# A mixture of experts whose scattered rows are gated first and added to one row of each token

## The chip, the cores and the metric

The kernel runs on one core of a Trainium2 chip. The metric is the device time of one execution, in microseconds (us). The core has TensorE (PE in the rows; PEld is its weight load), VectorE (DVE), ScalarE (ACT) and GpSimd (POOL), and SyncE (SP), which here only issues transfers. All transfers run on the core's 16 DMA engines.

## The reference, cut to what matters

One decoder layer: 512 tokens of 1024 numbers, two attention branches, and then 32 experts, of which each token takes 4. All the change lies in the experts' part:

```python
logits = xf @ w_router + b_router            # 512 x 32
vals, idx = lax.top_k(logits, 4)
gate = softmax(vals)                         # 512 x 4
# for every token and each of its 4 experts e:
up = x @ w_up[e] + b_up[e]                   # 2048 numbers: glu, lin
act = min(glu, 7) * sigmoid(1.702 * min(glu, 7)) * (clip(lin, -7, 7) + 1)
y = act @ w_down[e] + b_down[e]              # 1024 numbers
moe[token] += gate * y
out = x_mid + rmsnorm(moe) * g * (gate of the modulation)   # float32
```

## The kernel before, in words

**Stages.** Up to about 430 us attention, the router and the tables of places. Then a pipeline over 32 experts: at step i the up product of expert i (8 tiles of w_up, 1 MB each) and the down product of expert i-1 (4 tiles of w_down, 1 MB each). At the end the rows of each token are put together, normed, added to `xm` and stored.

**Kinds of experts.** The experts but the first are ranked by their number of rows. `KINDS` gives each step a number of slots: S has 128, N has 64, X has both. S is multiplied in three passes: `wsplit` splits a weight tile into `whi` (ACT) and `wlo` (DVE, both line 110), and `mm_w` (lines 1133 to 1141) multiplies. N is multiplied in plain float32 straight from `raw` (lines 1204 and 1258). A step over a pair N, S is the common case.

**Weights.** `parts` (line 1438) keeps `raw` tiles coming on SP's queue, through 9 buffers of 1 MB (`rawtile`): a load waits until its buffer has been consumed.

**Places.** `indices` (line 1057) turns the tables into three columns for each slot of an expert: the token `ti`, the row `di = 4 ti + j` of the token's j-th choice, and for N the half row `dh`. `gather` (line 1098) fetches the tokens' rows from DRAM, `scatter` (line 1228) writes an expert's result to rows of `y4`, a DRAM tensor of 2048 rows x 1024 (8 MB), that `zero_y4` cleared earlier. Both are issued by POOL. All experts' scatters write rows of their own, and the program declares that none waits for another.

**The end.** The last expert's result isn't scattered first: its rows are put in place on TensorE with a one-hot matrix `oht` (line 1604). For each of four blocks of 128 tokens (`q`), `partial` (line 1538) reads 2 MB of `y4`, and adds the four rows of a token, each multiplied by its gate `g4` (ACT line 1552, DVE line 1554). `finish` (line 1564) squares and sums (ACT), multiplies with `gp2` (POOL line 1569), works out the reciprocal root with small DVE operations (`rstd_of`, lines 218 to 231), scales and adds `xm` (DVE line 1571) and stores. A loop behind it, for experts with more rows than slots, closes the program.

**Order.** From step 2 on, `tc.manual_schedule` makes PE, ACT, DVE and POOL follow the order in which the code is written; before step 2 and after the last up step a scheduler sets it. SP's queue always follows the order of the code.

Of the kernel before, what the change touches and what calls it, by code (L numbers as in the profile page):

```python
# [20 lines left out]
S = 512  # L21
# [96 lines left out]
def emit(tc, A, dbg=None, stop_at=99):  # L118
# [194 lines left out]
    y4 = dram.tile([S * 4, D], F32, name="y4")  # L313

    def zero_y4(z, part):
        for i in part:
            k.load(y4[512 * i:512 * i + 512, :].rearrange("(p a) (b n) -> p (a b) n", p=128, n=256),
                   z[:, None, :].to_broadcast([128, 16, 256]))
# [524 lines left out]
    with tc.issue_after(k.last.ins):  # L843
        zero_y4(zero, range(4))
# [113 lines left out]
    g4 = rt.tile([128, NQ, 4], F32, name="g4")  # L958
# [6 lines left out]
    tab = rt.tile([128, NQ, 3, 32], BF16, name="tab")  # L965
# [6 lines left out]
    def route(qs):  # L972
        n, sl = len(qs), slice(qs[0], qs[-1] + 1)
        for q in qs:
            nc.vector.scalar_tensor_tensor(lg[:, q, :], pls[q], rn[1, q], br_, op0=OP.mult, op1=OP.add)
        for q in qs:
            nc.vector.max(v8[:, q], lg[:, q])
        for q in qs:
            nc.vector.max_index(i8[:, q], v8[:, q], lg[:, q])
        nc.vector.tensor_copy(i4[:, sl], i8[:, sl, 0:4])  # L980

        eoh = k.sp.tile([128, 2, n, 32, 4], F32, name=f"eoh{qs[0]}", tag="eoh", bufs=1)
        for i, q in enumerate(qs):
            nc.vector.tensor_tensor(eoh[:, 0, i], cst[:, C_E:C_E + 32][:, :, None].to_broadcast([128, 32, 4]),
                                    i4[:, q, None, :].to_broadcast([128, 32, 4]), op=OP.is_equal)
# [4 lines left out]
        return last  # L990
# [52 lines left out]
    scat = []  # L1043
# [13 lines left out]
    def indices(sets, tag, late=False):  # L1057
# [11 lines left out]
        di = rt.tile([128, n], I32, name="di" + tag, tag="di", bufs=3)  # L1069

        dh = rt.tile([128, n], I32, name="dh" + tag, tag="dh", bufs=3)

        def rest():
            pz = pq.tile([128, n, 4], F32, name=f"slot{tag}", tag="t")
            for i, parts in enumerate(sets):
                for pos_, vals, a, b in parts:
                    for q in range(NQ):
                        nc.tensor.matmul(pz[a:b, i, 0:3], lhsT=ohs[i][:, q, a:b], rhs=vals[:, q], start=(q == 0),  # L1078
                                         stop=(q == 3))
            sv = rt.tile([128, n, 3], F32, name="sv" + tag, tag="sv", bufs=2)  # L1080
            nc.vector.tensor_copy(sv, pz[:, :, 0:3])  # L1081
            nc.vector.scalar_tensor_tensor(ti, sv[:, :, 0], float(OOB), sv[:, :, 1], op0=OP.add, op1=OP.add)
            nc.vector.scalar_tensor_tensor(di, ti, 4.0, sv[:, :, 2], op0=OP.mult, op1=OP.add)
            return nc.vector.tensor_scalar(dh, di, 2.0, half, op0=OP.mult, op1=OP.add)
        return ti, di, dh, rest if late else rest()
# [142 lines left out]
    def scatter(ys, di):  # L1228
        h = D // ys.shape[1]
        st = nc.gpsimd.indirect_dma_start(out=y4.rearrange("r (h n) -> (r h) n", h=h) if h > 1 else y4,  # L1230
                                          out_offset=bass.IndirectOffsetOnAxis(ap=di, axis=0), in_=ys,
                                          in_offset=None, bounds_check=S * 4 * h - 1, oob_is_err=False)
        for s_ in scat:
            tc.declare_no_dep(st.ins, s_.ins, reason="every expert writes rows of its own")
        scat.append(st)

    class Down:
# [5 lines left out]
        def tile(self, c, raw, w):  # L1243
# [19 lines left out]
            if an is not None:  # L1263
                yn = etile("yn", 512)
                nc.scalar.activation(yn, self.pn, AF.Copy)
                after_tiles(2, lambda: scatter(yn, self.dis[1]))
            if a:
# [6 lines left out]
                nc.scalar.activation(ys, flat(self.p), AF.Copy)  # L1274
                after_tiles(2, lambda: scatter(ys, self.dis[0]))
# [7 lines left out]
    def tables():  # L1283
# [5 lines left out]
        nc.gpsimd.tensor_copy(byx[:, :, 1], tab[:, :, 2])  # L1289
# [116 lines left out]
    def prep(some, late=False):  # L1406
# [11 lines left out]
        ti, di, dh, last = indices(sets, f"s{some[0]}", late)  # L1418
        for n, (i, b) in enumerate(own):
            idx.setdefault(i, [None, None])[b] = (ti[0:64, n:n + 1], dh[:, n:n + 1]) if b else (ti[:, n:n + 1], di[:, n:n + 1])  # L1420
# [17 lines left out]
    def parts():  # L1438
# [9 lines left out]
        return ready.pop(0)  # L1448

# [17 lines left out]
    for i, kd in enumerate(KINDS):  # L1467
# [29 lines left out]
        for n, (c, x) in enumerate(tiles(i)):  # L1497
# [24 lines left out]
        if i + 1 < E:  # L1522
            down = Down(up, [x and x[1] for x in idx[i]], tags[1])
    by_hand.close()
    tick(True)


    def gp2_rows():
        g = xg0
        for j in range(2):  # L1530
            pz = ptile("gp2", "t")
            for b in range(4):
                nc.tensor.transpose(pz[:, 0, b * 128:(b + 1) * 128],
                                    colp[:, 2, 4 * j + b:4 * j + b + 1].to_broadcast([128, 128]), ident)
            nc.scalar.activation(g[:, j * 512:(j + 1) * 512], pz[:, 0], AF.Copy)
        return g

    def partial(q, y, more=False):

        yv = y4[q * 512:(q + 1) * 512, :].rearrange("(p j) d -> p j d", j=4)  # L1540
        yl = []
        for i in range(2):
            t = rawtile([128, 2, D])
            if q == NQ - 1 and i == 1:
                k.load(t[:, 0], yv[:, 2])
                k.load(t[:, 1], yv[:, 3])
            else:
                k.load(t, yv[:, 2 * i:2 * i + 2])
            yl.append(t)
        for j in range(4):  # L1550
            if j == 0 and not more:
                nc.scalar.activation(y, yl[0][:, 0], AF.Copy, scale=g4[:, q, 0:1])
            else:
                nc.vector.scalar_tensor_tensor(y, yl[j // 2][:, j % 2], g4[:, q, j:j + 1], y, op0=OP.mult, op1=OP.add)

    yqs = []

    def ytile(i):
        if i % 2 == 0:
            nb[0] += 1  # L1560
            yqs[:] = [ep.tile([128, 2, D], F32, name=f"yq{nb[0]}", tag=f"t{ysl[i // 2]}")]
        return yqs[0][:, i % 2]

    def finish(q, y, nm):

# [117 lines left out]
```

## Time and profile before

| | us |
|---|---|
| runs shown: lowest, median, highest | 1554.36, 1557.8, 1560.94 |
| the profiled execution | 1553.92 |
| its span | 1552.1 |
| last down matmul to the span's end | 1504.7 to 1552.1 |
| first scatter, last scatter that the reads wait for | 505.3, 1491.7 |

The span runs from the first to the last instruction of the profiled execution; 1.8 us of its time lie around it. TensorE is busy for 91% of it, DVE for 57%, and the DMA queue of SP for 76.6% of 16 engines. No single share tells what ends a stage: the experts' part has both TensorE and the DMA engines near full, and the chain of waits says which of them ended last.

### The profile page before, as it was taken

To read this page: it belongs to the slowest core of one execution; us is meant where nothing else is said; L and a number is where in the kernel's file an instruction comes from. 1 tells how busy PE (TensorE), PEld (TensorE's weight loads), DVE (VectorE), ACT (ScalarE), POOL (GpSimd) and SP (SyncE) were. 2 spreads that over 40 slices of the span, in tenths; PEclk is the share of its full clock that TensorE was granted. 3 is DMA by queue.
4 is the path that set the end of the run, shared out by engine and by line. 5 is a ranking of instruction groups with operands and counts; after the bars stand their busy time and mean duration, and the time that the engine had idled before them with its cause. 6 is when DMAs were issued, how large, how long until landed. Compare 5 with 4: busy or idle time off the path is not lost.

```text
span 1552.1 us, 19027 instructions
## 1 busy us (share of the span) xinstructions
PE 1417.7 (91%) x6949; PEld 906.5 (58%) x6949; DVE 879.4 (57%) x1290; ACT 671.4 (43%) x826; POOL 158.9 (10%) x190
## 2 busy tenths in 40 slices
PE   7999999998868999999979999999999999899980
PEld 2788785576745656657435445756647556474550
DVE  2786747766877454736333343754736547463566
ACT  3545435465544443635232242543625526252441
POOL 0200020100342000000010110000000000000002
PEclk9999999999869999999999999999999999999995
DMA  8522137308676999999996999999999999999972
GB/s 299 169 82 82 56 129 274 139 28 271 244 248 263 376 404 420 411 412 411 420 404 240 385 376 419 416 416 419 416 414 415 415 406 417 405 391 415 420 303 104
DMA packets 101798, 494.17 MB, mean 318 GB/s; under 512 B 14353, under 2 KB 39418, under 8 KB 48579
## 3 DMA queue, kind: packets, MB, share of 16 engines
q1 hardware_dynamic: 93139, 472.12, 76.6%
q0 software_dynamic: 8560, 20.78, 3.8%
q8 instruction: 56, 0.92, 0.2%
q14 instruction: 43, 0.35, 0.1%
HBM read 474.50 MB, written 26.74 MB: 323 GB/s over the span
## 4 chain that ended last, share of the span: by engine, by line
PE 71%; DVE 12%; DMA 10%; ACT 5%; issue 2%; SPq 0%; ACTq 0%; DVEq 0%; POOLq 0%
PE un L1204 9%; PE dnn L1258 7%; DMA raw<-in_w_down_dram 6%; PE ug L1137 4%; PE ug L1139 4%; PE ul L1137 4%; PE ul L1139 4%; PE ug L1141 3%; PE ul L1141 3%; DVE wlo L110 3%; PE dn L1141 3%; PE dn L1137 3%; DMA raw<-in_w_up_dram 2%; PE dn L1139 2%; ACT whi L110 2%
## 5 line engine op out<-in xcount | busy, mean ns | idle before, releaser
L110 DVE TENSOR_TENSOR wlo<-raw,whi 128x2048 fp32r<-128x2048 f32 x180 | 408.2, 2291 | 130.9 <-ACT whi L110 130.4
L110 ACT ACTIVATE whi<-raw 128x2048 fp32r<-128x2048 f32 x180 | 342.5, 1914 | 125.6 <-PE ul L1139 41.9
L1204 PE MATMUL un<-raw,xn 128*64 128x512 f32 x1152 | 259.7, 599 | 0.0
L1204 PEld LDWEIGHTS un<-raw,xn 128*64 128x64 f32 x1152 | 79.2, 137 | 152.3 <-issue 151.3
L1258 PE MATMUL dnn<-raw,an 128*64 128x512 f32 x576 | 132.6, 599 | 2.2 <-DMA raw<-in_w_down_dram 2.2
L1141 PE MATMUL dn<-wlo,at 128*128 128x512 f32 x240 | 78.1, 407 | 10.3 <-DVE wlo L110 9.6
L110 ACT ACTIVATE xt<-xT 128x1024 fp32r<-128x1024 f32 x15 | 15.3, 1023 | 164.6 <-PE xT L1113 164.6
L1137 PE MATMUL ug<-whi,xt 128*128 128x512 f32 x240 | 79.4, 412 | 3.7 <-ACT whi L110 2.5
L1137 PE MATMUL dn<-whi,at 128*128 128x512 f32 x240 | 78.4, 408 | 3.2 <-ACT whi L110 2.7
L1258 PEld LDWEIGHTS dnn<-raw,an 128*64 128x64 f32 x576 | 37.7, 136 | 72.0 <-issue 64.6
L1081 DVE COPY svs<-slots 128x6 f32<-128x6 f32 (+2 forms) x17 | 2.8, 164 | 134.6 <-PE slots L1078 134.6
L1137 PE MATMUL ul<-whi,xt 128*128 128x512 f32 x240 | 77.2, 402 | 1.6 <-DVE ln L1175 1.6
L1141 PE MATMUL ug<-wlo,xt 128*128 128x512 f32 x240 | 76.0, 398 | 1.9 <-DVE wlo L110 1.9
L1139 PE MATMUL ug<-whi,xt 128*128 128x512 f32 x240 | 77.5, 404 | 0.0
L1139 PE MATMUL ul<-whi,xt 128*128 128x512 f32 x240 | 77.0, 402 | 0.0
L1139 PE MATMUL dn<-whi,at 128*128 128x512 f32 x240 | 75.6, 396 | 0.0
L1141 PE MATMUL ul<-wlo,xt 128*128 128x512 f32 x240 | 75.5, 396 | 0.0
L1099 POOL DMA_INDIRECT xg<-h2d,tis x33 | 37.0, 1121 | 364.6 <-PE xN L1124 219.2
L1174 DVE TENSOR_SCALAR l<-ul 128x1024 f32<-128x1024 f32 x15 | 18.3, 1223 | 86.2 <-PE ul L1146 86.2
L1141 PEld LDWEIGHTS dn<-wlo,at 128*128 128x128 f32 x240 | 43.2, 188 | 28.9 <-DVE wlo L110 20.2
L112 DVE SCALAR_TENSOR_TENSOR at<-aT,at 128x1024 fp32r<-128x1024 f32 x15 | 18.4, 1225 | 72.7 <-ACT at L111 72.7
L1137 PEld LDWEIGHTS dn<-whi,at 128*128 128x128 f32 x240 | 42.9, 189 | 24.0 <-ACT whi L110 11.2
(521 smaller groups left out, 2483.9 us busy)
## 6 DMA issues: line engine op xcount, KB each, us to landing
raw<-in_w_up_dram SPq DMA_DIRECT2D x256, 1024.0 KB, 17.4
raw<-in_w_down_dram SPq DMA_DIRECT2D x127, 1024.0 KB, 16.2
wada<-in_w_ada_dram SPq DMA_DIRECT2D x24, 1024.0 KB, 7.3
y<-zero SPq DMA_DIRECT2D x4, 2048.0 KB, 16.6
raw<-y SPq DMA_DIRECT2D x7, 1024.0 KB, 11.9
wor<-in_w_out_dram SPq DMA_DIRECT2D x4, 1024.0 KB, 6.0
x<-in_x_dram SPq DMA_DIRECT2D x8, 256.0 KB, 5.2
xm<-in_x_dram SPq DMA_DIRECT2D x4, 512.0 KB, 5.7
```

Source lines behind the costliest of these rows:

```text
L110: return (nc.scalar.activation(hi, src, AF.Copy), nc.vector.tensor_sub(lo, src, hi.bitcast(F32)))
L112: nc.vector.scalar_tensor_tensor(lo, src, scale, hi.bitcast(F32), op0=OP.mult, op1=OP.subtract))
L1081: nc.vector.tensor_copy(sv, pz[:, :, 0:3])
L1099: k.last = nc.gpsimd.indirect_dma_start(out=xg0[0:n], out_offset=None, in_=h2d, in_offset=bass.IndirectOffsetOnAxis(ap=ti[0:n], axis=0), b ...
L1137: nc.tensor.matmul(o, lhsT=xh, rhs=wh, start=first, stop=False)
L1139: nc.tensor.matmul(o, lhsT=xl, rhs=wh, start=False, stop=False)
L1141: nc.tensor.matmul(o, lhsT=xh, rhs=wl, start=False, stop=False)
L1174: nc.vector.tensor_scalar(l, pl_, 8.0, -6.0, op0=OP.min, op1=OP.max)
L1204: nc.tensor.matmul(self.pn[64 * c:64 * c + 64, a], lhsT=xn[:, kk, :], rhs=raw[:, o:o + 512], start=False, stop=kk == KT - 1, skip_group_ch ...
L1258: nc.tensor.matmul(self.pn[64 * n:64 * n + 64], lhsT=an[:, c % 2 * 2 + b, 64 * (c // 2):64 * (c // 2) + 64], rhs=raw[:, b, 512 * n:512 * n ...
```

## The change

Each token has one row in DRAM, `ytot` (512 x 1024, 2 MB), where it had four. ACT multiplies an expert's rows with their gates as it moves them out of PSUM, and the scattering transfer adds them to the row in DRAM (`compute_op=OP.add`). For that the gate travels through the tables: `tab` has five columns in place of three (the token's two parts, and the gate in three bf16 parts, `in_three`), and `indices` gives a column of gates `gs_`. The declaration that scatters don't wait for each other is gone: each waits for the one before. The end reads the 2 MB of `ytot` in four loads of 512 KB, and TensorE adds them, through the identity in float32, to the one-hot product of the last expert. ACT squares from PSUM, DVE multiplies from PSUM with the root and `gp2`, and adds `xm` in a second operation; POOL does nothing there. The one-hot matrix and `gp2` are made at the last up step's sixth tile. The hand-written order now covers the end, too.

```diff
-    y4 = dram.tile([S * 4, D], F32, name="y4")
+    ytot = dram.tile([S, D], F32, name="ytot")
+    def zero_y(z):
+        k.load(ytot.rearrange("(p a) (b n) -> p (a b) n", p=128, n=256), z[:, None, :].to_broadcast([128, 16, 256]))
...
-        zero_y4(zero, range(4))
+        zero_y(zero)
...
-        last = nc.vector.tensor_reduce(mb[:, sl], eoh[:, 0], op=OP.max, axis=AX.X)
-        nc.vector.tensor_tensor(eoh[:, 1].rearrange("p n e j -> p (n e) j"), eoh[:, 0].rearrange("p n e j -> p (n e) j"),
-                                cst[:, C_J:C_J + 4][:, None, :].to_broadcast([128, n * 32, 4]), op=OP.mult)
-        nc.vector.tensor_reduce(tab[:, sl, 2], eoh[:, 1], op=OP.max, axis=AX.X)
+        return nc.vector.tensor_reduce(mb[:, sl], eoh, op=OP.max, axis=AX.X)
...
+    nc.vector.tensor_tensor(gw, lg, v8[:, :, 0:1].to_broadcast([128, NQ, 32]), op=OP.subtract)
+    nc.scalar.activation(gw, gw, AF.Exp)
+    nc.vector.tensor_tensor(gw, gw, mb, op=OP.mult)
+    nc.vector.tensor_reduce(gs4, gw, op=OP.add, axis=AX.X)
     nc.vector.reciprocal(gs4, gs4)
+    nc.vector.tensor_tensor(gw, gw, gs4[:, :, None].to_broadcast([128, NQ, 32]), op=OP.mult)
+    def in_three(dst, src, r):
+        nc.vector.tensor_copy(dst[:, :, 0], src)
+        nc.vector.tensor_tensor(r, src, dst[:, :, 0], op=OP.subtract)
+        nc.vector.tensor_copy(dst[:, :, 1], r)
+        nc.vector.tensor_tensor(r, r, dst[:, :, 1], op=OP.subtract)
+        nc.vector.tensor_copy(dst[:, :, 2], r)
+    in_three(tab[:, :, 2:5], gw, gr)
...
-            nc.vector.scalar_tensor_tensor(di, ti, 4.0, sv[:, :, 2], op0=OP.mult, op1=OP.add)
-            return nc.vector.tensor_scalar(dh, di, 2.0, half, op0=OP.mult, op1=OP.add)
+            nc.vector.tensor_reduce(gs_, sv[:, :, 2:5], op=OP.add, axis=AX.X)
+            return nc.vector.tensor_scalar(dh, ti, 2.0, half, op0=OP.mult, op1=OP.add)
...
     def scatter(ys, di):
         h = D // ys.shape[1]
-        st = nc.gpsimd.indirect_dma_start(out=y4...,
-                                          bounds_check=S * 4 * h - 1, oob_is_err=False)
-        for s_ in scat:
-            tc.declare_no_dep(st.ins, s_.ins, reason="every expert writes rows of its own")
+        nc.gpsimd.indirect_dma_start(out=ytot...,
+                                     bounds_check=S * h - 1, oob_is_err=False, compute_op=OP.add)
...
-                nc.scalar.activation(ys, flat(self.p), AF.Copy)
-                after_tiles(2, lambda: scatter(ys, self.dis[0]))
+                nc.scalar.activation(ys, flat(self.p), AF.Copy, scale=self.dis[0][1])
+                after_tiles(2, lambda: scatter(ys, self.dis[0][0]))
...
+    def y_rows():
+        for q in range(NQ):
+            if q % 2 == 0:
+                t = rawtile([128, 2, D])
+            k.load(t[:, q % 2], ytot[q * 128:(q + 1) * 128, :])
+    def finish(q, y, nm, z, gp2):
+        nc.scalar.activation(z, y, AF.Square, accum_out=ssf)
+        r = rstd_of(ssf, D, f"rf{nm}{q}")
+        nc.vector.scalar_tensor_tensor(z, y, r, gp2, op0=OP.mult, op1=OP.mult)
+        nc.vector.tensor_tensor(z, z, xm[q], op=OP.add)
+        k.load(A["out"][0, q * 128:(q + 1) * 128, :], z)
...
+            if i == E - 1 and n == 5:
+                oht, gp2 = one_hots(), gp2_rows()
...
+    def first(q):
+        for n in range(2):
+            nc.tensor.matmul(pcs[q][:, n], lhsT=ident, rhs=ys[q][:, n * 512:(n + 1) * 512], start=True, stop=False)
+    for q in range(NQ - 1):
+        first(q)
+    for q in range(NQ):
+        if q == NQ - 1:
+            first(q)
+        for n in range(2):
+            for i in range(2):
+                nc.tensor.matmul(pcs[q][:, n], lhsT=oht[:, q], rhs=yr[:, i, n * 512:(n + 1) * 512], start=False, stop=(i == 1))
+    for q in range(NQ):
+        finish(q, flat(pcs[q]), "", ys[q], gp2)
+    by_hand.close()
+    scatter(yl, ti)
```

POOL's queue around the step of kind X, before. `xg` is a gather's tile, `y` and `yn` are what is scattered, and the brackets name what an instruction waits for (DMASW are semaphores of transfers that POOL issued).

```order
L1230 DMA y_380<-yn_6794,dhs_5820 4096x512 [waits Activation_49]
L1474 COPY cm_6984<-sel 128x128 [waits PE_49,Pool_49]
L1099 DMA xg_3889<-h2d,tis_6607 128x1024 [waits DMASW5_49,DMASW3_49]
L1230 DMA y_380<-yn_6978,dhs_6229 4096x512 [waits Activation_49]
L1230 DMA y_380<-y_6982,dis_6228 2048x1024 [waits DMASW7_49,Activation_49]
L1099 DMA xg_3889<-h2d,tis_7021 64x1024 [waits DMASW5_49,DVE_49,PE_49]
```

The same place in the changed kernel:

```order
L1235 DMA ytot<-yn_6804,dhs_5829 1024x512 [waits DMASW2_49,Activation_49]
L1515 COPY cm_6994<-sel 128x128 [waits PE_49,Pool_49]
L1104 DMA xg_3886<-h2d,tis_6617 128x1024 [waits DMASW3_49]
L1235 DMA ytot<-yn_6988,dhs_6238 1024x512 [waits DMASW4_49,Activation_49]
L1235 DMA ytot<-y_6992,tis_6237 512x1024 [waits DMASW6_49,Activation_49]
L1104 DMA xg_3886<-h2d,tis_7031 64x1024 [waits DMASW5_49,DVE_49,PE_49]
```

The instructions stand in the same order; what moved is the wait: every scatter now waits for a transfer of POOL's queue, too, the scatter before it.

DVE's queue during the first up step, before: `wlo` is the split of a weight tile, `svs` and `tis` lead to the second expert's gather.

```order
L110 TENSOR_TENSOR wlo_4452<-raw_3881,whi_4451 128x2048
L1330 TENSOR_SCALAR pos_4403<-pos_4403 128x4
L1065 TENSOR_TENSOR ohs_4425<-cst,pos_4403 128x4x64 x2
L1065 TENSOR_TENSOR ohs_4428<-cst,pos_4403 128x512
L110 TENSOR_TENSOR wlo_4468<-raw_3883,whi_4467 128x2048
L1081 COPY svs_4446<-slots_4433 128x6
L1065 TENSOR_TENSOR ohs_4642<-cst,pos_4403 128x4x64
L1082 SCALAR_TENSOR_TENSOR tis_4430<-svs_4446 128x2
```

The same stretch in the changed kernel:

```order
L1069 TENSOR_TENSOR ohs_4438<-cst,pos_4408 128x512
L1028 TENSOR_TENSOR gr<-gr,tab_4409 128x128
L110 TENSOR_TENSOR wlo_4478<-raw_3880,whi_4477 128x2048
L1029 CAST tab_4409<-gr 128x4x32
L110 TENSOR_TENSOR wlo_4494<-raw_3882,whi_4493 128x2048
L1085 COPY svs_4444<-slots_4443 128x10
L110 TENSOR_TENSOR wlo_4510<-raw_3884,whi_4509 128x2048
L1087 SCALAR_TENSOR_TENSOR tis_4440<-svs_4444 128x2
```

Two more splits of a weight tile stand ahead of `tis`, and the five operations of `in_three` are threaded between.

PE's queue after the last down matmul, in the changed kernel (`sum` are the PSUM tiles of the four blocks, `raw` the loaded rows of `ytot`, `cst` the identity):

```order
L1151 MATMUL dn_10750<-bt,sel 128x512 x2
L1586 MATMUL sum_10818<-raw_10781,cst 128x512 [waits DMAHW2_49]
L1586 MATMUL sum_10818<-raw_10781,cst 128x512
L1586 MATMUL sum_10819<-raw_10781,cst 128x512 [waits DMAHW3_49]
L1586 MATMUL sum_10819<-raw_10781,cst 128x512
L1586 MATMUL sum_10820<-raw_10784,cst 128x512 [waits DMAHW4_49]
L1586 MATMUL sum_10820<-raw_10784,cst 128x512
L1594 MATMUL sum_10818<-yr,oht 128x512 [waits Activation_49]
```

Six float32 matmuls now stand between the last down matmul and the first one-hot matmul, which came right behind it before.


## Rows read from the trace of the kernel before

**Rows 1.** Page, 40 slices of 38.8 us: DMA engines' busy tenths.

```profile
DMA  8522137308676999999996999999999999999972
```

**Rows 2.** Windows: start, end, length, each engine's busy us, granted clock, DMA share, GB/s.

```profile
505.00:780.00 275.00, 267.78 (x1268) 160.54 (x1266) 138.79 (x104) 113.32 (x82) 19.98 (x23) 1.00 1.01 409
780.00:900.00 120.00, 108.37 (x485) 52.55 (x483) 39.45 (x32) 33.49 (x28) 13.45 (x11) 0.97 0.86 334
900.00:1436.00 536.00, 521.21 (x2451) 316.46 (x2449) 289.15 (x248) 233.83 (x164) 40.21 (x43) 1.00 1.01 412
```

**Rows 3.** Chain that ended last, experts' part: start, us, engine, work, records.

```profile
551.04 10.45 PE un L1204 x48
...
613.45 10.45 PE un L1204 x48
...
740.09 15.88 DMA raw<-in_w_down_dram
...
1081.42 14.78 DMA raw<-in_w_down_dram
...
1145.29 14.35 DMA raw<-in_w_down_dram
```

**Rows 4.** Page, DMA queue of POOL's transfers: packets, MB, share of 16 engines.

```profile
q0 software_dynamic: 8560, 20.78, 3.8%
```

**Rows 5.** Source line 1230: issue ns min/median/max, first and last start; landing times.

```profile
L1230 POOL DMA_INDIRECT y<-yn,dhs x18: 1007/1080/2461, 551.3 to 1491.7; - x18
L1230 POOL DMA_INDIRECT y<-y,dis x15: 992/1010/1101, 505.3 to 1534.6; - x15
DMA to landing us min/median/max: 3.2/7.8/10.0
```

**Rows 6.** Timeline of POOL: start, us, line, operation; in brackets idle before, and releaser.

```profile
472.01 2.69 POOL L1099 DMA_INDIRECT xg<-h2d,tis  x1 [0.83 <-PE ul L1139]
...
505.29 1.01 POOL L1230 DMA_INDIRECT y<-y,dis  x1 [22.92 <-DVE dhs L1084]
...
771.07 1.00 POOL L1230 DMA_INDIRECT y<-y,dis  x1 [19.58 <-ACT y L1274]
...
896.29 1.02 POOL L1230 DMA_INDIRECT y<-yn,dhs  x1 [13.10 <-ACT yn L1265]
...
908.89 0.97 POOL L1099 DMA_INDIRECT xg<-h2d,tis  x1 [10.29 <-PE xT L1113]
...
1430.60 1.00 POOL L1230 DMA_INDIRECT y<-y,dis  x1 [16.43 <-ACT y L1274]
...
1491.66 2.42 POOL L1230 DMA_INDIRECT y<-yn,dhs  x1 [29.75 <-ACT yn L1265]
```

**Rows 7.** Timeline of DVE before the first gather: start, us.

```profile
434.76 0.41 DVE L989 TENSOR_REDUCE tab<-eoh 128x64 bf16<-128x256 f32 x1
```

**Rows 8.** Page, costliest groups: the split of a weight tile on DVE.

```profile
L110 DVE TENSOR_TENSOR wlo<-raw,whi 128x2048 fp32r<-128x2048 f32 x180 | 408.2, 2291 | 130.9 <-ACT whi L110 130.4
```

**Rows 9.** Timeline of PE behind the second gather.

```profile
480.20 0.68 PE L1124 MATMUL xN<-cst,xg 64*128 64x64 f32 x8 [1.42 <-DMA xg<-h2d,tis]
...
482.73 0.85 PE L1195 MATMUL un<-bt,cm 128*128 128x512 f32 x2 [1.84 <-DVE l L1174]
```

**Rows 10.** Timeline of all engines, the end.

```profile
1504.04 0.63 PE L1146 MATMUL dn<-bt,sel 128*128 128x512 f32 x2
...
1507.04 3.58 PE L1604 MATMUL comb<-yr,oht 128*128 128x512 f32 x13 [0.30 <-DVE yr L110]
...
1511.67 1.05 ACT L1568 ACTIVATE scrf<-yq 128x1024 f32<-128x1024 f32 x1
...
1537.91 1.28 DVE L1571 SCALAR_TENSOR_TENSOR yq<-yq,rf_r,xm 128x1024 f32<-128x1024 f32 x1 [0.46 <-DVE rf_r L231]
```

**Rows 11.** Lines, the end's window: xcount, busy us, mean ns, idle before.

```profile
L230 DVE TENSOR_SCALAR rf_u<-rf_u,rf_t 128x1 f32<-128x1 f32 x8 | 1.6, 205 | 0.0
L228 DVE TENSOR_SCALAR rf_u<-rf_t 128x1 f32<-128x1 f32 x8 | 1.2, 147 | 0.0
```

More of the change, by code (lines that the diff above doesn't have):

```diff
@@ L1417, in prep @@
                 own.append((i, 1))
-        ti, di, dh, last = indices(sets, f"s{some[0]}", late)
+        ti, gs_, dh, last = indices(sets, f"s{some[0]}", late)
         for n, (i, b) in enumerate(own):
-            idx.setdefault(i, [None, None])[b] = (ti[0:64, n:n + 1], dh[:, n:n + 1]) if b else (ti[:, n:n + 1], di[:, n:n + 1])
+            idx.setdefault(i, [None, None])[b] = (ti[0:64 if b else 128, n:n + 1], (dh if b else ti)[:, n:n + 1], gs_[:, n:n + 1])
         return last
@@ L1522, in emit @@
         if i + 1 < E:
-            down = Down(up, [x and x[1] for x in idx[i]], tags[1])
-    by_hand.close()
+            down = Down(up, [x and x[1:] for x in idx[i]], tags[1])
     tick(True)
[L1528 to L1554, printed above, removed]
@@ L1591, in emit @@
     for c, x in tiles(E):
-        down.tile(x, *parts())
-    py = pys[0]
-    yq = [ytile(q) for q in range(NQ)]
-    for q in range(2):
-        partial(q, yq[q])
-    yr = ep.tile([128, 2, D], F32R, name="yr", tag=f"t{[x for x in free if x not in ysl][0]}")
-    yh, yl_ = yr[:, 0], yr[:, 1]
-    k.split(yh, yl_, py)
+        w = parts()
+        if x == 2:
+            ys = y_rows()
+        down.tile(x, *w)
+    py, = pys
+    ti, _, gs_ = idx[E - 1][0]
+    yr = ep.tile([128, 2, D], F32R, name="yr", tag=f"t{free[0]}")
+    k.split(yr[:, 0], yr[:, 1], py, gs_)
+    yl = etile("l")
+    nc.scalar.activation(yl, py, AF.Copy, scale=gs_)
+    pcs = [ptile("sum", ("uA", "uB", "t", "dn")[q]) for q in range(NQ)]
+    def first(q):
[3 more added lines that the diff above has]
+        first(q)
     for q in range(NQ):
-        pc = ptile("comb", ("uA", "uB", "t", "uA")[q])
+        if q == NQ - 1:
+            first(q)
         for n in range(2):
-            for i, w in enumerate((yh, yl_)):
-                nc.tensor.matmul(pc[:, n], lhsT=oht[:, q], rhs=w[:, n * 512:(n + 1) * 512], start=(i == 0), stop=(i == 1))
-        pc = pc.rearrange("p a n -> p (a n)")
-        if q < 2:
-            nc.vector.scalar_tensor_tensor(yq[q], pc, gl[:, q, 4:5], yq[q], op0=OP.mult, op1=OP.add)
-        else:
-            nc.scalar.activation(yq[q], pc, AF.Copy, scale=gl[:, q, 4:5])
-    for q in range(NQ):
-        if q > 1:
-            partial(q, yq[q], True)
-        finish(q, yq[q], "")
-    ys = etile("y")
-    nc.scalar.activation(ys, py, AF.Copy)
-    scatter(ys, di)
+            for i in range(2):
+                nc.tensor.matmul(pcs[q][:, n], lhsT=oht[:, q], rhs=yr[:, i, n * 512:(n + 1) * 512], start=False, stop=(i == 1))
+    for q in range(NQ):
+        finish(q, flat(pcs[q]), "", ys[q], gp2)
+    by_hand.close()
+    scatter(yl, ti)
     free[:] = [0, 1, 2]
-    ysl = [0, 1]
     selx, xrow = xs
@@ L1649, in emit @@
             tick(True)
-        gp2_rows()
-        yq = [ytile(q) for q in range(NQ)]
-        for q in range(NQ):
-            partial(q, yq[q])
-            finish(q, yq[q], "2")
+        gp2 = gp2_rows()
+        for q, y in enumerate(y_rows()):
+            finish(q, y, "2", etile("y"), gp2)
     es.close()
```

114 lines of the change are left out of this document (49 added, 65 removed).

## The prediction

> **What bounds the kernel now.** I read the page's 40 slices first, then windows over the experts' part, then the chain of waits in it, then single timelines at the places that the change touches.
>
> The slices show the DMA engines at nine tenths or more in nearly every slice from about 505 us on, with one dip, and at six to eight tenths between 349 and 505 us [rows 1]. The windows say the same with numbers: from 505 to 780 us and from 900 to 1436 us the engines are busy all the time (share 1.01, 409 and 412 GB/s), and between, 780 to 900 us, the share is 0.86 [rows 2]. TensorE is full beside them: 267.78 of 275 us and 521.21 of 536 us [rows 2]. So the two are nearly balanced, and the chain has to say which ends last. Two steps of a pair N, S begin at 551.04 and 613.45, 62.4 us apart, with no transfer between them in the chain: there TensorE sets the pace, and the nine buffers of weights still hold a reserve. Then the chain has 15.88 us of a transfer of w_down at 740.09: the reserve is gone. Later such a transfer stands once in each pair: 1081.42 and 1145.29 are 63.9 us apart [rows 3]. So the pace of the experts' part is the DMA engines', by about 1.5 us a pair; work added to them there lengthens the kernel nearly one for one, while work taken from them could give back only that 1.5 us a pair.
>
> The end is another matter: from the last down matmul (1504.04) to the last multiplication of DVE (1537.91, ended 1539.2) no large transfer is waited for, and the path is DVE's [rows 10].
>
> **The change part by part.**
>
> *Adding in place of writing.* A scatter that adds must have the row that lies in DRAM, too. All tokens' rows together are 2048 x 4 KB = 8.39 MB, so at most that much is fetched in addition. No row of before shows an adding transfer; I bound it. From below: nothing, if the fetch lies beside the write and the engines' time is that of the write alone. From above: two more passes over the rows, one for the fetch and one for the addition. The nearest row is POOL's own queue, which gathers and scatters just such rows: 20.78 MB in 3.8% of 16 engines [rows 4], that is 0.038 x 1552.1 = 59 us of all sixteen, 2.84 us a MB. One more pass over 8.39 MB is then 23.8 us. (By the rate of the full stretches, 412 GB/s [rows 2], it would be 20.4.) I take one pass, the price of a gather of the same rows, since the fetch is one.
>
> How much of it shows? There are 33 scatters, 18 and 15 [rows 5]. Nine are issued from 505.29 to 771.07 and 19 from 896.29 to 1430.60 [rows 6], in the stretches whose DMA share is 1.01; the two between lie in the dip, which has about 0.14 x 120 = 17 us to spare [rows 2], and three come at the end. So 23.8 x 28 / 33 = **20 us**, with ends 0 and 40. In the first stretch the reserve of buffers takes it up until 740, and then the wait there is that much longer.
>
> The Trainium skill ("Collectives: The Full Stack", section "The bandwidth ceiling: the fold count and why AG ≠ RS ≠ AR") says that an adding transfer is slow not for the addition but because it reads two sources through the same ring, and gives a measured ratio of 1.93 to a copy. As an estimate from that page the addition would cost 0.93 of a pass, 19 us in place of 20, and the kernel about 1 us less than my sum. No run of before shows it; it speaks against the change just as my nearest row does.
>
> *Scatters that wait for each other.* A scatter lands 7.8 us after its issue in the median, 10.0 at most [rows 5]. What it waits for now is some 30 us old in the steps of pairs, since a pair of 62.4 us has two. Only in the step of kind X do two stand one behind the other (896.29, and the next in the order), with a gather behind both; there the second now waits the landing, 8 to 10 us, POOL's queue behind it with it. That gather was issued at 908.89, 12.6 us after the first of them and released by PE [rows 6]; so 2 to 4 us of reserve. I put 0 to it, and up to +5 if the landing doubles.
>
> *Zero fill.* 8 MB become 2 MB. The fill runs before the router's chain, where the slices from 349 to 505 us are at six to eight tenths [rows 1], so the transfers of weights beside it had room already, and attention's last products and the router's DVE work cover it. Nothing, or at most 1 us gained.
>
> *Front.* Four DVE operations of about 0.41 us go before the tables (the last at 434.76 [rows 7]), so the first gather comes about 1 us earlier. In the first up step, two more splits of a weight tile, 2.29 us each [rows 8], and the five small operations of the gate's parts stand before the second expert's `tis`; its gather (472.01 [rows 6]) comes perhaps 3 us later, and the matmuls that wait for it at 480.20 too. But the matmul behind these, at 482.73, waited for DVE [rows 9] anyway, so 2 of the 3 stay on the path. Sum **+1 us**, from -1 to +4.
>
> *End.* The loads of the rows wait for the scatter at 1491.66 [rows 6], issued when the weights are nearly all in; such a one lands 3.2 us later at the least [rows 5], at 1495. They are 2 MB now, about 5 us at 412 GB/s and some more to land, and are there by about 1504, when the last down matmul ends at 1504.7 [rows 10]. Then six float32 matmuls through the identity. The float32 matmuls of `un` run in 10.45 us for 48 records, 0.218 each, two column halves side by side, two records a matmul [rows 3]; a full-width one is thus four times 0.218, 0.87 us, and six are 5.2: 1509.9. The first block's four one-hot matmuls are 4 x 3.58 / 13 = 1.1 [rows 10]: 1511.0. ACT's square, 1.05 [rows 10], and its hand-over: about 1512.3. DVE then does for each of four blocks eleven 128 x 1 operations of 0.147 to 0.205 [rows 11], 1.9 us together, and two of full width, each about the 1.28 of the multiplication at 1537.91 [rows 10]: 4.4 a block, 17.6 in all, so it ends at 1530 where it ended at 1539.2. The additions of gated rows on DVE and the multiplication on POOL are gone; what is late next is DVE alone. The store and the closing loop behind it stay. **-9 us**; -4 if the float32 matmuls take twice that.
>
> *Gates on ACT, one-hots and `gp2` at the last up step.* The scale rides on a copy that ACT did already, and the moved operations stand where TensorE works on the last up product: 0, at most +2.
>
> *Sum.* +20 + 1 - 9 = +12 on the profiled execution's 1553.9 (span 1552.1 and 1.8 around it): **1566**. The median of the runs shown is 3.9 above that execution, so 1570 against it.
>
> **The rivals.**
>
> *The fetch is hidden.* If an adding transfer holds an engine no longer than a plain one, only the front and the end count: 1553.9 + 1 - 9 = 1546, not slower. For it: POOL's queue is only 3.8% of the engines [rows 4], and the engines' busy share may contain waiting for memory in which a second fetch fits. Against it: 409 to 412 GB/s in both full stretches whatever the mix [rows 2] looks like a limit of the engines. It decides if the extra costs below 8/23.8 = a third to 40% of a pass.
>
> *More than a pass.* If the fetch and the addition each take a pass of their own, 40 in place of 20: 1553.9 + 40 + 1 - 9 = 1586. The X step's wait would then bite as well. Against it: nothing in the rows asks for a second pass.
>
> *The end loses its gain.* The loads stand behind the last scatter. If that lands not 3 to 4 but 13 us after 1491.66, the loads land at about 1513 in place of 1504, the identity matmuls follow them, and the -9 is gone: 1553.9 + 20 + 1 = 1575. For it: landings reach 10.0 us under load [rows 5]. Against it: at 1491.66 few weights are left to load, and the minimum of the landings is 3.2 [rows 5].
>
> **How the numbers follow.** One pass: 0.50, 1566, its own range 1557 to 1577 (0.7 to 1.2 passes, front and end within their bounds). Hidden: 0.30, 1546. More than a pass: 0.12, 1586. The end without its gain: 0.08, 1575. 0.5%, about what a measurement of this kernel can tell from no change, is 7.8 us, so the second case lies on the line: of its 0.30 I put 0.21 to faster, 0.09 to no change. Of the first case, 0.12 falls within 0.5%, when the front is free and the pass is cheap; with a hundredth of it faster, 0.37 is slower. So faster 0.22, same 0.21, slower 0.37 + 0.12 + 0.08 = 0.57. The range 1546 to 1585 cuts off somewhat less than half of the hidden case and half of the dear one.
>
> **What would show it.** POOL's queue should show about 59 + 24 us of 16 engines, 5.3% of the span, with its bytes up by at most 8.4 MB. The later pairs should be 65.3 us apart in place of 63.9 (two scatters' worth, 1.4 us), the wait of the chain near 740 longer by 6 us, and the up step of the last expert about 20 us later. The last down matmul to DVE's last large operation should take 25 us, where it took 34.5. Pairs that stay at 63.9 us and an unchanged share of POOL's queue would prove the forecast wrong; so would a last pair that ends on time with a longer end.

## The result, and the profile after

| | us |
|---|---|
| kernel before, 4 runs | 1556.08 (1553.72 to 1560.94) |
| changed kernel, 4 runs | 1571.63 (1570.85 to 1572.85) |
| ratio | 1.009, interval 1.0064 to 1.0116 |
| its profiled span | 1570.1 |

The change makes the kernel 0.9% slower, some 15 us. The profiled spans differ by 18.0. The table takes them apart at five marks: `pos` is a small DVE operation behind the experts' tables (L1330 before, L1333 after), then the first scatter, the end of the last down matmul, the end of DVE's last addition of `xm`, and the span's end.

| stretch | before | after | difference | forecast |
|---|---|---|---|---|
| start to `pos` | 460.0 | 462.0 | +2.0 | -1 |
| `pos` to first scatter | 45.3 | 52.3 | +7.0 | +2 |
| first scatter to last down matmul | 999.4 | 1019.5 | +20.2 | +20 |
| last down matmul to DVE's last | 34.5 | 26.8 | -7.7 | -9 |
| DVE's last to span's end | 12.9 | 9.5 | -3.4 | 0 |

The mark `pos` in the kernel before:

```profile
460.00 0.17 DVE L1330 TENSOR_SCALAR pos<-pos 128x4 f32<-128x4 f32 x1
```

The first line of the table can't be told from scatter between executions: in two later kernels, whose code up to there is that of the kernel before, `pos` stood at 464.4 and 465.3. Behind `pos` the stretches of the changed kernel came out the same to a few tenths in a second execution (after_again below), so from here on stretches are compared, not starts.

**The experts' part.** The page's line on POOL's queue, after (before: [rows 4]):

```profile
q0 software_dynamic: 9712, 20.79, 5.3%
```

The bytes are the same: if the addition fetches the rows, they are not counted in them. But the engines' time went from 3.8% of 1552.1 to 5.3% of 1570.1, 59 to 83 us. The chain of waits in that part, after, with the wait of [rows 3] now from the first pair on:

```profile
561.77 10.47 DMA raw<-in_w_down_dram
...
757.42 17.58 DMA raw<-in_w_down_dram
...
1040.57 17.78 DMA raw<-in_w_down_dram
...
1105.40 17.68 DMA raw<-in_w_down_dram
```

Scatters by line, after (as [rows 5]), and some of them on POOL's timeline (as [rows 6]):

```profile
L1235 POOL DMA_INDIRECT ytot<-yn,dhs x18: 1569/1592/2934, 560.2 to 1522.1; - x18
L1235 POOL DMA_INDIRECT ytot<-y,tis x14: 1563/1566/1826, 514.3 to 1457.3; - x14
DMA to landing us min/median/max: 5.0/9.7/12.3
```

```profile
514.28 1.64 POOL L1235 DMA_INDIRECT ytot<-y,tis  x1 [21.55 <-ACT y L1276]
...
786.70 1.59 POOL L1235 DMA_INDIRECT ytot<-y,tis  x1 [19.56 <-ACT y L1276]
...
912.83 1.61 POOL L1235 DMA_INDIRECT ytot<-yn,dhs  x1 [13.16 <-ACT yn L1267]
...
918.57 1.57 POOL L1235 DMA_INDIRECT ytot<-y,tis  x1 [4.13 <-DMA ytot<-yn,dhs]
...
970.84 1.59 POOL L1235 DMA_INDIRECT ytot<-yn,dhs  x1 [14.52 <-DVE ohs L1069]
...
1427.69 1.57 POOL L1235 DMA_INDIRECT ytot<-yn,dhs  x1 [15.01 <-ACT yn L1267]
...
1457.27 1.59 POOL L1235 DMA_INDIRECT ytot<-y,tis  x1 [16.47 <-ACT y L1276]
```

The scatter of before that stands where 970.84 is:

```profile
954.30 1.07 POOL L1230 DMA_INDIRECT y<-yn,dhs  x1 [14.87 <-DVE ohs L1065]
```

A landing takes 9.7 us in place of 7.8, and an issue 1.6 in place of 1.0. Only one scatter waits for the one before it, 4.13 us in the step of kind X. From 970.84 to 1427.69 are seven pairs, 65.3 us each, where [rows 3] has 63.9.

**The front.** DVE ahead of the second gather, that gather on POOL, and the matmul that waits for it on PE, after:

```profile
461.98 0.17 DVE L1333 TENSOR_SCALAR pos<-pos 128x4 f32<-128x4 f32 x1
...
466.84 4.97 DVE L110 TENSOR_TENSOR wlo<-raw,whi 128x2048 fp32r<-128x2048 f32 x1 [0.55 <-ACT whi L110]
...
471.81 5.52 DVE L110 TENSOR_TENSOR wlo<-raw,whi 128x2048 fp32r<-128x2048 f32 x1
477.25 0.15 DVE L1087 SCALAR_TENSOR_TENSOR tis<-svs 128x2 int32<-128x2 f32 x1
```

```profile
465.08 10.10 POOL L1059 TENSOR_TENSOR bt<-braw,bt 32x1536 fp32r<-32x1536 f32 x2 [6.33 <-ACT bt L1057]
478.22 5.96 POOL L1104 DMA_INDIRECT xg<-h2d,tis  x1 [3.03 <-DVE dhs L1089]
```

```profile
490.32 1.09 PE L1129 MATMUL xN<-cst,xg 64*128 64x64 f32 x8 [10.81 <-DMA xg<-h2d,tis]
```

The two splits ahead of `tis` do not take 2.29 us each [rows 8] but 4.97 and 5.52, as long as POOL subtracts `bt` beside them. Counted from `pos`, the gather's issue begins 4.2 us later (16.2, before 12.0) and takes 3.3 longer (5.96, 2.69 in [rows 6]), so it ends 7.5 us later. TensorE stands idle for 10.81 ahead of the matmul that needs it (1.42 in [rows 9]); in all of the stretch up to the first scatter it is idle for 12.1 us, where it was for 5.1, and that is the 7.0 but for a tenth.

**The end.** PE and DVE, after (as [rows 10]):

```profile
1533.18 0.63 PE L1151 MATMUL dn<-bt,sel 128*128 128x512 f32 x2
1533.65 5.31 PE L1586 MATMUL sum<-raw,cst 128*128 128x512 f32 x12
1538.40 3.33 PE L1594 MATMUL sum<-yr,oht 128*128 128x512 f32 x12
```

```profile
1543.47 1.28 DVE L1487 SCALAR_TENSOR_TENSOR raw<-sum,rf_r,xg 128x1024 f32<-128x1024 f32 x1
...
1548.33 1.28 DVE L1487 SCALAR_TENSOR_TENSOR raw<-sum,rf_r,xg 128x1024 f32<-128x1024 f32 x1
...
1559.36 1.23 DVE L1488 TENSOR_TENSOR raw<-raw,xm 128x1024 f32<-128x1024 f32 x1
```

The identity matmuls follow the last down matmul at once, so the loaded rows were there. DVE sets the pace, 4.86 us a block.

### The profile page after: what moved, and what is told of

It is laid out like the page before. It is cut to its first block, busy times and chain, and to the rows that moved or that the text cites. A ratio compares the mean times of both kernels' runs of the same rounds, so it can differ in the third digit from the quotient of the medians.

```text
span 1570.1 us, 19039 instructions
## 1 busy us (share of the span) xinstructions
PE 1430.1 (91%) x6973; PEld 914.0 (58%) x6973; DVE 861.1 (55%) x1284; ACT 670.5 (43%) x822; POOL 197.2 (13%) x186
## 3 DMA queue, kind: packets, MB, share of 16 engines
q0 software_dynamic: 9712, 20.79, 5.3%
## 4 chain that ended last, share of the span: by engine, by line
PE 48%; DMA 15%; DVE 4%; ACT 2%; issue 1%; DVEq 0%; ACTq 0%
DMA raw<-in_w_down_dram 11%; PE un L1209 7%; PE dnn L1260 7%; PE ug L1142 4%; PE ul L1142 3%; PE ug L1144 3%; PE ug L1146 3%; PE ul L1144 3%; PE ul L1146 3%; PE dn L1146 3%; DMA raw<-in_w_up_dram 3%; PE dn L1142 2%; PE dn L1144 2%; DVE wlo L110 2%; ACT whi L110 1%; PE aT L1118 1%
## 5 line engine op out<-in xcount | busy, mean ns | idle before, releaser
L110 DVE TENSOR_TENSOR wlo<-raw,whi 128x2048 fp32r<-128x2048 f32 x180 | 414.6, 2328 | 150.7 <-ACT whi L110 150.4
L1104 POOL DMA_INDIRECT xg<-h2d,tis x33 | 44.6, 1351 | 327.5 <-PE xN L1129 191.2
L110 ACT ACTIVATE xt<-xT 128x1024 fp32r<-128x1024 f32 x15 | 15.4, 1024 | 163.3 <-PE xT L1118 163.3
L1085 DVE COPY svs<-slots 128x10 f32<-128x10 f32 (+3 forms) x19 | 3.2, 166 | 135.1 <-PE slots L1083 135.0
L1235 POOL DMA_INDIRECT ytot<-yn,dhs x18 | 34.2, 1897 | 278.7 <-ACT yn L1267 148.1
## 6 DMA issues: line engine op xcount, KB each, us to landing
raw<-in_w_up_dram SPq DMA_DIRECT2D x256, 1024.0 KB, 16.1
```

Source lines behind the costliest of these rows:

```text
L110: return (nc.scalar.activation(hi, src, AF.Copy), nc.vector.tensor_sub(lo, src, hi.bitcast(F32)))
L1085: nc.vector.tensor_copy(sv[:, :, v], pz[:, :, v])
L1104: k.last = nc.gpsimd.indirect_dma_start(out=xg0[0:n], out_offset=None, in_=h2d, in_offset=bass.IndirectOffsetOnAxis(ap=ti[0:n], axis=0), b ...
L1235: nc.gpsimd.indirect_dma_start(out=ytot.rearrange("r (h n) -> (r h) n", h=h) if h > 1 else ytot, out_offset=bass.IndirectOffsetOnAxis(ap=d ...
```

## The experiments

In the table `pos` to scatter, scatter to matmul and matmul to DVE are the stretches above; the ratio is to the kernel before, with its interval.

| kernel | `pos` to scatter | scatter to matmul | matmul to DVE | median | ratio |
|---|---|---|---|---|---|
| before | 45.3 | 999.4 | 34.5 | | |
| changed | 52.3 | 1019.5 | 26.8 | 1571.63 | 1.009 (1.0064 to 1.0116) |
| changed, again | 52.3 | 1019.2 | 26.8 | 1573.24 | 1.0103 (1.0083 to 1.0123) |
| e1_plain | 52.1 | 999.9 | 26.8 | 1557.52 | 1.0001 (0.9988 to 1.0014) |
| e2_add_own | 45.3 | 1019.6 | 38.2 | 1580.04 | 1.0147 (1.0122 to 1.0173) |
| e3_waits | 45.4 | 999.4 | 35.9 | 1557.95 | 1.0013 (0.9999 to 1.0026) |
| e4b_one_part | 45.0 | 1019.5 | 26.8 | 1568.76 | 1.0071 (1.0047 to 1.0095) |
| e5_bias_dve | 46.5 | 1017.9 | 26.8 | 1569.77 | 1.008 (1.0061 to 1.01) |
| e7_tis_first | 48.0 | 1019.9 | 26.8 | 1569.9 | 1.0091 (1.0073 to 1.011) |
| e6_before_bias | 43.1 | 997.1 | 34.2 | 1552.39 | 0.9984 (0.997 to 0.9998) |
| h1 | 44.5 | 997.9 | 35.2 | 1553.11 | 0.9984 (0.9971 to 0.9996) |
| h2 | 42.9 | 998.9 | 36.0 | 1555.78 | 0.9997 (0.9985 to 1.001) |
| h2_bias | 45.1 | 996.8 | 36.3 | 1551.0 | 0.997 (0.9958 to 0.9982) |
| h3_bias | 45.6 | 997.4 | 36.3 | 1551.83 | 0.9972 (0.9958 to 0.9987) |

**e1_plain: no addition.**

```diff
-                                     bounds_check=S * h - 1, oob_is_err=False, compute_op=OP.add)
+                                     bounds_check=S * h - 1, oob_is_err=False)
```

> The changed kernel with plain scatters: rows overwrite in place of being added (so the sums of experts are left out of the output), every wait kept. Theory (the addition makes the DMA engines fetch the rows as well, in stretches where they set the pace): first to last stage 20 us shorter, 1571.6 - 20 = about 1552; POOL's queue back from 5.3% to 3.8% of 16 engines; the pairs of steps back from about 65.2 to 63.9 us. Rival (the scatters' waits for each other and POOL's longer issue cost it): stays at 1571, within 3. Rival (the later second gather starves the whole experts' part): stays at 1571, too. In every case the front's 9 us and the shorter end remain.

Its queue, first scatter and last down matmul:

```profile
q0 software_dynamic: 8560, 20.78, 3.8%
```

```profile
516.64 1.02 POOL L1235 DMA_INDIRECT ytot<-y,tis  x1 [21.76 <-ACT y L1276]
```

```profile
1515.95 0.63 PE L1151 MATMUL dn<-bt,sel 128*128 128x512 f32 x2
```

From the scatter to the end of that matmul 999.94: the 19.6 us are gone with the addition, the waits stayed. The median fell by 14, less than the stretch, since the last stretch grew to 12.4 and starts scatter.

**e2_add_own: the addition alone, in the kernel before.**

```diff
-                                          in_offset=None, bounds_check=S * 4 * h - 1, oob_is_err=False)
+                                          in_offset=None, bounds_check=S * 4 * h - 1, oob_is_err=False, compute_op=OP.add)
```

> The kernel before, with its scatters adding in place of writing (each to rows of its own, which were cleared, so the output is the same); no wait is added. Theory (extra fetch): 1556 + 20 = about 1576, POOL's queue at about 5.3% and pairs at 65.2 us. Rival (the waits, not the additions): 1556, within 3. If a row's addition costs more where it is not ordered: over 1580.

Its queue, first scatter, last down matmul, and two rows of its chain near the end:

```profile
q0 software_dynamic: 9712, 20.79, 5.3%
```

```profile
510.60 1.64 POOL L1230 DMA_INDIRECT y<-y,dis  x1 [22.91 <-DVE dhs L1084]
```

```profile
1529.60 0.63 PE L1146 MATMUL dn<-bt,sel 128*128 128x512 f32 x2
```

```profile
1517.20 5.11 DMA y<-yn,dhs
...
1522.44 5.19 DMA raw<-y
```

The stretch is 1019.6, 20.2 above that of before: the addition alone does it. The time, 1580, is 4 us above the 1576 expected and on the mark that I had set for additions that cost more where no order holds them; but these cost the same 20.2, and what is more stands in the end, which is 3.7 us longer. There the chain goes through the last scatter and a load of the rows, which the chain of before has not: the rival of the late loads is real, in the kernel that reads 8 MB.

**e3_waits: the waits alone.** The declaration of independence (the loop over `scat`) is taken out of the kernel before.

> The kernel before, where each scatter waits for the one before it as in the changed kernel; nothing else changes. Theory: the scatters are 30 us apart and land in under 10, so the waits are over before they begin: 1556, within 3, with perhaps 1 us in the step of kind X. Rival (waits cost it): 1565 to 1576.

First scatter, last down matmul:

```profile
509.70 1.01 POOL L1230 DMA_INDIRECT y<-y,dis  x1 [22.98 <-DVE dhs L1084]
```

```profile
1508.45 0.63 PE L1146 MATMUL dn<-bt,sel 128*128 128x512 f32 x2
```

The stretch is 999.4 to the tenth, with one wait of 4.23 us in the step of kind X. The end is 1.4 longer, with a load of the rows in its chain, too; the time is the same within its interval. The waits cost nothing where the DMA engines set the pace.

**e4b_one_part: DVE's old order at the second gather.**

```diff
-        nc.scalar.activation(gw, pv[:, :, 1], AF.Copy)
-        in_three(tab2[:, :, 2:5], gw, gr)
+        nc.scalar.activation(tab2[:, :, 2], pv[:, :, 1], AF.Copy)
+        nc.gpsimd.memset(tab2[:, :, 3:5], 0.0)
```

> The changed kernel where the second table holds the gate in one bf16 part only (the two finer parts are left out, so the gates of all experts but the first are rounded): DVE's order before the second gather is then that of the kernel before, with tis behind one split of a weight tile less, and without the five small operations. Theory (the second gather is late because tis stands behind those splits, and everything behind it moves by that): the second gather comes 6 us earlier and the time falls by 6 to 9, to about 1564. Rival (the lateness is absorbed by the reserve of nine buffers, and the whole 20 and more come from the additions): within 2 of 1571.6.

```profile
466.68 0.17 DVE L1333 TENSOR_SCALAR pos<-pos 128x4 f32<-128x4 f32 x1
...
474.38 3.48 DVE L1087 SCALAR_TENSOR_TENSOR tis<-svs 128x2 int32<-128x2 f32 x1
```

The first scatter:

```profile
511.67 1.64 POOL L1235 DMA_INDIRECT ytot<-y,tis  x1 [22.81 <-ACT y L1276]
```

On DVE `tis` begins 7.7 us behind `pos`, not 15.3, and the stretch to the first scatter is 45.0: all 7 us are back, and the experts' part stays at 1019.5, so the reserve of weights takes up none of it. The median does not show them: it is 2.9 us below the changed kernel's, where I had expected 6 to 9, and the intervals overlap; `pos` stands at 466.7 in the profiled execution, 4.7 later than in the changed kernel's.

**e5_bias_dve: the changed order, without POOL beside it.** In `bias_rows`, `nc.gpsimd.tensor_tensor(bt[o], ...)` becomes `nc.vector.tensor_tensor`.

> The changed kernel with one operation on another engine: the rest of the bias rows (bt, two subtractions of 32x1536) is taken by DVE in place of POOL. In the changed kernel POOL's 10.1 us of it stand beside two splits of a weight tile that took 4.97 and 5.52 us on DVE where 2.29 is usual, ahead of the second expert's tis and gather, and the gather's own issue took 5.96. Theory (the two engines hold each other up there): the splits take 2.3 again, the bias on DVE adds 3 to 4, the second gather is issued some 3 us earlier and takes 2.7: from the bias to the first scatter 43 to 46 us in place of 49.2, the whole about 1567. Rival (DVE's order alone is the cause): 49 to 52 us there, time 1571 to 1574.

```profile
468.37 0.16 DVE L1333 TENSOR_SCALAR pos<-pos 128x4 f32<-128x4 f32 x1
...
476.27 2.28 DVE L110 TENSOR_TENSOR wlo<-raw,whi 128x2048 fp32r<-128x2048 f32 x1
...
478.55 2.28 DVE L110 TENSOR_TENSOR wlo<-raw,whi 128x2048 fp32r<-128x2048 f32 x1
480.75 0.15 DVE L1087 SCALAR_TENSOR_TENSOR tis<-svs 128x2 int32<-128x2 f32 x1
```

```profile
481.69 2.37 POOL L1104 DMA_INDIRECT xg<-h2d,tis  x1 [16.12 <-DVE gss L1088]
...
514.85 1.64 POOL L1235 DMA_INDIRECT ytot<-y,tis  x1 [22.40 <-ACT y L1276]
```

With the same splits ahead of `tis`, each takes 2.28 again, though DVE's 3.53 us for the two subtractions stand there now as well; the gather is issued 2.9 us earlier behind `pos` and its issue takes 2.37. 5.8 of the 7.0 us are back. So the loss needs both: the splits ahead, and POOL's subtraction beside them. In the median 2 to 3.5 us are to be seen, and the intervals overlap with the changed kernel's; about 1567 was expected.

**after_again and e7_tis_first.** The first is the changed kernel unaltered; the second passes `in_three` into `indices`, which calls it behind `tis`:

```diff
+                    if mid:
+                        mid()
...
-        in_three(tab2[:, :, 2:5], gw, gr)
...
-        prep([E0, E0 + 1])
+        prep([E0, E0 + 1], False, lambda: in_three(tab2[:, :, 2:5], gw, gr))
```

> The changed kernel once more, unaltered, as the measure for the next run on the same chip: 1.0% above the kernel before. From the fifth expert place table (pos) to the first scatter 52.3 us, first scatter to last down matmul 1018.9, end 26.8, as in its first profile; what differs between executions should lie ahead of the tables.

> The changed kernel with the second table's gate parts made after the second expert's tis: the columns of places are fetched by a first group of matmuls, tis follows, and only then in_three and the columns of gates. On DVE tis stands behind one split of a weight tile fewer than three, as in the kernel before; nothing is left out. Theory (the front's loss of 7 us is the order ahead of tis, and passes in full to the end): from pos to first scatter about 45 us in place of 52.3, the rest unchanged, 7 us below the run above on the same chip, about 0.45%. Rival (the reserve of weights takes the front's delay up): the first scatter earlier by 7, but the experts' part longer by as much; time equal within 2.

In e7_tis_first, DVE, PE and the first scatter:

```profile
458.31 0.16 DVE L1334 TENSOR_SCALAR pos<-pos 128x4 f32<-128x4 f32 x1
...
465.86 0.15 DVE L1087 SCALAR_TENSOR_TENSOR tis<-svs 128x2 int32<-128x2 f32 x1
```

```profile
472.48 0.59 PE L1083 MATMUL slots<-tab,ohs 128*64 128x3 bf16 x12 [4.98 <-DVE tab L1029]
...
473.93 1.05 PE L1148 MATMUL ul<-wlo,xt 128*128 128x512 f32 x2
```

```profile
506.29 1.64 POOL L1237 DMA_INDIRECT ytot<-y,tis  x1 [21.34 <-ACT y L1278]
```

`tis` begins 7.6 us behind `pos`, but the first scatter comes 4.3 us earlier, not 7. The median is 3.3 lower, which the intervals don't separate. The other 3 us stand on TensorE: the wait for the gather is gone, but the matmuls that fetch the columns of gates now wait 4.98 us for the last operation of `in_three`: on DVE its second operation took 3.54 us beside POOL's subtraction, and its last ends at 472.4. Behind that wait, from 472.5 to 478.2, the granted clock is 0.50, the lower of its two levels (1.2 GHz), and a pair of matmuls takes 1.05 us, where it takes 0.63 at the clock of 1.00 from 478.2 on.

**e6_before_bias: the edit of e5 on the kernel before.**

> The same edit on the kernel before: the subtraction of the bias rows on DVE. There POOL's 7.94 us stood beside ohs and tis, which took 3.69 and 3.49 in place of 0.4 and 0.2. Theory: tis comes 2 to 4 us earlier for the shorter operations, less what a split more ahead of it takes: from 42.0 us (bias to first scatter) to between 39 and 42, the whole 1554 to 1557. Rival (DVE is full there, so 3 to 4 us more on it delay everything): 44 to 46 us and 1559 to 1561.

It is faster by 0.16%, by its interval just clear of none, and its first two stretches are 2.2 and 2.3 us shorter.

**h1, h2, h2_bias, h3_bias: the old scatters with an end on TensorE.** They keep the four rows of each token and their plain scatters; two rows are added on TensorE through a diagonal matrix of their gates, ACT gates a third, DVE adds the fourth:

```diff
+                nc.tensor.matmul(pcs[q][:, n], lhsT=dg[:, q, j], rhs=ys[4 * q + j][:, n * 512:(n + 1) * 512],
+                                 start=(j == 0), stop=False)
...
+        nc.scalar.activation(a, a, AF.Copy, scale=g4[:, q, 2:3])
+        nc.vector.scalar_tensor_tensor(a, b_, g4[:, q, 3:4], a, op0=OP.mult, op1=OP.add)
```

> A mixture: front, tables and plain scatters to four rows of each token as in the kernel before, and an end in the changed kernel's manner. TensorE adds two of a token's four rows through a diagonal matrix of their gates, ACT and DVE gate and add the other two, the last expert's rows are gated as they leave PSUM, the one-hots, gp2 and the diagonals are made at the last up step or beside the last down tiles, DVE multiplies with gp2 and adds xm, and POOL does nothing. Theory (the change's only gain is the end, and its costs are the additions and the front): experts' part as before (998.7 us from first scatter to last down matmul), the end about 29 us in place of 34.5, the whole about 1551. Rival (the end waits for the 8 MB of rows, not for DVE): end 34 us or more, 1556 and up.

> The mixture again, with the end in another order: in the first mixture ACT's square of block 0 stood behind the gating of block 2's rows, whose load landed at 1514.8, so DVE's first finishing operations began at 1517, and a copy for the closing loop stood ahead of the gatings. Here each block's square and finishing stand ahead of the next block's rows. Theory (the rows' loads are no bound if nothing queues behind them): first to last operation of the end about 28 us from the last down matmul, where the kernel before has 34.5 and the first mixture 35.2; the whole about 1549. Rival (8 MB of rows at the end set the pace, so the gain of the changed kernel's end needs its 2 MB): 33 us or more, 1553 or more.

> The same with the subtraction of the bias rows on DVE in place of POOL. Theory (the gain of that edit on the kernel before, 0.16%, adds to the end's): 2 to 3 us below the run above, about 1546. Rival (that gain was the scatter between executions): the same as the run above, within 1.

> The mixture with the bias rows on DVE, and the gating of blocks 2 and 3 ahead of the finishing of block 1 (in the run before this their gating stood behind ACT's squares, and TensorE waited 5.5 us for DVE in the middle of the end, which took 36.2 us). Theory: the end takes 29 to 31 us, 5 to 7 less than that run's 36.2, the whole about 1546, 0.5 to 0.7% below the kernel before. Rival (the loads of 8 MB are what the end waits for): 34 us and more, 0.3% below as the run before.

All four ends took 35 to 36 us: for three of them I had expected 28 to 31, and for h2_bias a time of 1546 that rests on the same; all four were wrong. In h2_bias, PE:

```profile
1504.21 0.62 PE L1150 MATMUL dn<-bt,sel 128*128 128x512 f32 x2
...
1523.52 3.78 PE L1653 MATMUL sum<-raw,cst 128*128 128x512 f32 x4 [5.59 <-DVE rf_v L218]
```

TensorE waits for DVE in the middle, and h3_bias, which meant to lift that, has the same wait (5.58). The loads of the 8 MB are not what holds it there: in h2_bias TensorE waits 0.16 us for them behind the last down matmul. So moving additions to TensorE did not give the shorter end of the changed kernel, in any of the four orders; that it needs rows that come gated and added is likely but not shown, since another order might lift the wait. h2_bias and h3_bias still beat the kernel before, by 0.3%; by their marks only 2.7 and 1.7 us ahead of the end are theirs, against 1.8 lost in it, so where the rest of their 4 us comes from stays open.

## Why the prediction was right, and where not

**One extra pass over the rows: right, and its price shown.** +20 forecast; 20.2 in the changed kernel, 19.6 taken away by e1_plain, 20.2 brought by e2_add_own. POOL's queue was forecast at 5.3% and is. That the extra time is a fetch stays the prediction's account: the runs show the time and 1152 more packets, but no bytes. The rule of the Trainium skill ("Collectives: The Full Stack", section "The bandwidth ceiling: the fold count and why AG ≠ RS ≠ AR"), whose 1.93 was measured between two collectives and not on a scatter, would have given 19; the runs lie at or a little above it and don't tell the two apart. Rivals that hide the fetch, or double it, fall.

**Its places: half right.** Between the marks of [rows 6] the nine scatters up to 786.70 cost 6.6 us (272.42 for 265.78), as 9 x 0.72. From 912.83 to 1457.27 the stretch is 10.1 longer (544.44 for 534.31), not 13.7: up to 970.84 nothing is added (58.01 in both); a reserve of weights filled in the dip would explain it, but it was not tested. From there each pair costs 1.4. Of the missing 3.6, 3.4 are found in the dip (+0.9) and behind 1457.27 (+2.5), where I had put none. That the sum came out to the tenth is luck. Nor did the first stretch go as I wrote: the reserve did not last until 740. Nothing is added up to 622.54 (108.3 us behind the first scatter, 108.4 before), 1.8 us are added by the fifth scatter (654.56) and 6.8 by the seventh (721.85), and the wait near 740 is not 6 us longer but 1.7 (17.58 for 15.88).

**Waits between scatters: right.** e3_waits adds nothing in the experts' part; the one wait of 4.13 us fell into the reserve of the step of kind X.

**Front: the step that failed.** I priced two splits at 2.29 each and let 2 of 3 us stay on the path, with +4 as the upper end of the front's sum; it is +7.0. The order was read correctly, the price was not: I took a duration from a row of all 180 splits, for a place where POOL's subtraction runs. Also, I left the gather's issue at its 2.69, and it took 5.96. Of the 1 us that the first gather was to come earlier, 0.2 are there: counted from one of POOL's operations ahead of the router (401.87 and 403.71) it comes 37.7 and 37.5 us later. The kernel before showed the sign of the long splits at that place, on POOL and on DVE:

```profile
463.24 7.94 POOL L1055 TENSOR_TENSOR bt<-braw,bt 32x1536 fp32r<-32x1536 f32 x2 [6.16 <-ACT bt L1053]
```

```profile
464.10 3.69 DVE L1065 TENSOR_TENSOR ohs<-cst,pos 128x256 bf16<-128x256 f32 x1
467.71 3.49 DVE L1082 SCALAR_TENSOR_TENSOR tis<-svs 128x2 int32<-128x2 f32 x1
```

`ohs` takes 0.41 elsewhere in that timeline, and `tis` 0.15 in the changed kernel. Two small operations sat out POOL's two; in the changed kernel two splits sit them out, and `tis` comes behind. e4b_one_part and e5_bias_dve each take one half of the cause away and get back 7.3 and 5.8. The Trainium skill ("SBUF — State Buffer", section "Terms") says that DVE and GpSimd hold a shared port pair by an exclusive lock, for the whole of an instruction; the stretched splits agree with it. For the 5.96 us of the gather's issue it is not shown: in e5_bias_dve that stands beside splits on DVE, too, and takes 2.37.

**End: right in kind, 1.3 us short.** -7.7 for -9. The six identity matmuls took 5.31 us of records (5.2 forecast); a block on DVE takes 4.86, not 4.4: beside its 1.28 and 1.23 the eleven small operations take 2.4 from start to end, not the 1.9 of their own durations. The rows were loaded in time.

**Last stretch: not foreseen.** It is 9.5 us in all kernels with the changed end and the adding scatter, 12.4 in e1_plain, 12.9 before. In e2_add_own, with the old end, it is 11.6. The stores look alike; why the addition shortens it was not found.

**Sum.** +20.2 + 7.0 - 7.7 - 3.4 = +16.1, and +2.0 ahead of `pos`, give the 18.0 between the profiled spans (to rounding); the forecast was +12, and the time lies within its range. That it is not further off is luck in part: the last stretch, for which I had put nothing, gives back more than half of what the front's price left out.

## What to carry to other kernels

A scatter that adds cost the DMA engines here about the time of a gather of the same rows: price it by what POOL's queue already takes for a gather, and count it where the DMA engines set the pace. A duration is read at the place where the instruction will stand, with what runs on the neighbouring engine there, not from a mean over the kernel. Compare executions between marks: what lies ahead of them scattered here by more than the effect of an edit.

## What the runs showed that was not expected

- The extra time of an adding scatter shows in no count of bytes: POOL's queue has 20.78 and 20.79 MB, with 8560 and 9712 packets, and e2_add_own reads as much from memory as the kernel before, 474.50 MB.
- An adding scatter takes POOL 1.6 us to issue, a plain one 1.0.
- Executions of the same code differ by 4 to 5 us ahead of `pos` (460.0, 464.4, 465.3), and from there to the last down matmul by a few tenths (45.3 and 45.4, 999.4 and 999.4; the changed kernel 1019.5 and 1019.2).
